# A transformer block on one Trainium2 core: a fifth group of seven-product tiles in the down projection, with its weight sums, sums of products and convolution taps moved to other engines

## The chip, the cores and the metric

The program runs on one core of a Trainium2 chip. The metric is the device time of one execution in microseconds. Time before: 970.25 us, the median of 3 runs (969.86 to 970.68).

In the profile PE is TensorE's matmul, PEld its weight load, DVE is VectorE, ACT is ScalarE, POOL is GpSimd, and SP is the engine that issues most DMAs; a name with q is that engine's queue.

## The reference

One encoder block over x of 256 tokens by 2048 features, in float32: RMSNorm and one input projection, windowed attention of 12 heads beside a Fourier group, an output projection with a residual add, then the feed-forward part, to which the change belongs, and a last RMSNorm:

```python
def _conv_ffn(h, w_up, dw_w, dw_b, w_down):
    up = h @ w_up
    gate, val = up[..., :D_FF], up[..., D_FF:]
    gate = lax.conv_general_dilated(      # centred, width 3, one filter per feature
        gate, dw_w, window_strides=(1,), padding=((CONV_WIDTH // 2, CONV_WIDTH // 2),),
        dimension_numbers=('NWC', 'WIO', 'NWC'), feature_group_count=D_FF) + dw_b
    act = jax.nn.gelu(gate, approximate=False) * val
    return act @ w_down
...
        x = x + _conv_ffn(_rmsnorm(x, norm2_g), w_up, dw_w, dw_b, w_down)
    return _rmsnorm(x, normf_g)
```

D_FF is 5504, which is 43 tiles of 128 features. w_up is 2048 x 11008, w_down 5504 x 2048.

## The kernel before

Every float32 matmul is made of three matmuls on rounded parts. A matrix is split into hi, its value rounded to the matmul type (written by ScalarE), and lo, the rest (raw minus hi, on VectorE); the product sums hi x hi, hi x lo and lo x hi in PSUM. Weights come by DMA in units of 128 x 2048 (1 MB) into three raw buffers, and each unit is split once (`split`, L163 and L164, or `split_product`, L905 and L906 for the groups below). There are three hi and three lo buffers, so unit n+2 is split while unit n is on TensorE.

The feed-forward part is a list of items, made by `ff_items`, that TensorE works off in order. An item of kind gate or val is one up-projection tile (16 k tiles, 32 matmuls, of 512 and 256 columns in turn). A product is 12 matmuls of 512 columns, and a late ("down") item is 24 of them. `ff_step(n)`, called behind the matmuls of item n, issues the work of the other engines in this order: the posts beside item n (those that follow item n-1, and the second step of n-2), then the split of item n+2, then the posts behind item n. All queues run in the order of issue, which is fixed by hand.

The posts of a gate tile: `scaled_sum` (ScalarE copies half of the PSUM result, VectorE adds the other half and multiplies by the token scale r2b), `gate_conv` (ScalarE writes the middle tap and the bias into cv, VectorE adds the two outer taps, L809 and L812), and `gate_gelu` on ScalarE. Of a val tile: `scaled_sum` and `val_mult`, which multiplies by the gate.

The down projection of tiles 0 to 31 is done in 4 groups of 8 tiles by a 2 x 2 block scheme with seven products instead of eight (Strassen's, in the form that needs few sums). The blocks are: two halves of 4 k tiles, two halves of 128 tokens, and output columns c and c+2 of the four column blocks of 512; so each group has two halves c = 0, 1 of 7 products, P1, P2, N3, N4, N5, P6, P7. On the activation side `operand` and `operand_sums` make seven operands per group. On the weight side four blocks a, b, c, d (1 MB each) are loaded into a ring of two buffers (`ring_load`), and sums are made in a buffer x (tag sumw, one buffer): `first_sums` writes x = a+b on VectorE and has a DMA of GpSimd's queue add d onto b in place; after the split of N5 an accumulating DMA adds d onto x, and after P6 another adds c. P1 uses a, P7 b+d, N5 a+b, N3 d, P6 a+b+d, P2 c, N4 a+b+d+c.

The order of products is P1, P7, N5, N3, P6, P2, N4 for c = 0 and P1, N5, P7, N3, P6, P2, N4 for c = 1. PATTERN sets them between the up items of the next 8 tiles: three up items, then product and up item in turn.

`product_out` takes a product out of PSUM on VectorE: it is added onto the output rows xs and onto the shared sums U, N5 and P7 in SBUF, up to two additions for a product. `shared_out`, once per half, folds the shared sums into xs.

Tiles 32 to 39 are done plainly (three matmuls each) by 8 "down" items (LATE), tiles 40 to 42 by the four last items, whose results go through `last_post` (add to xs, square sum). `gain` multiplies by normf_g on GpSimd, `finish` scales by the row norm and stores the output in four pieces for each half of the tokens. PSUM has eight banks: four for up items (mm) and four for products and the rest (dn).

Of the kernel before, what the change touches and what calls it, by code (L numbers as in the profile page):

```python
# [13 lines left out]
P = 128  # L14
# [39 lines left out]
N_GROUPS = 4  # L54
LATE = [list(range(32, 36)), list(range(36, 40))]
# [5 lines left out]
PATTERN = "uuu" + "su" * 13 + "s"  # L61


def ff_items():


    def ups(tiles):
        return [(kind, j) for j in tiles for kind in ("gate", "val")]

    items = ups(range(8))  # L70
    for g in range(N_GROUPS):
        todo = {
            "u": ups(range(8 * g + 8, 8 * g + 16)),
            "s": [("product", g, c, p) for c in range(2) for p in PRODUCTS[c]],
        }
        items += [todo[c].pop(0) for c in PATTERN]
        assert not any(todo.values())
    items += [("down", 0, c) for c in range(4)] + ups(LAST)
    items += [("down", 1, c) for c in range(4)] + [("last", c) for c in range(4)]
    return items  # L80
# [3 lines left out]
def block_kernel(  # L84
# [9 lines left out]
    w_down: bass.AP,  # L94
    w_down_late: bass.AP,
# [25 lines left out]
    for n, it in enumerate(items):  # L121
        if it[0] == "product":
            continue
        up_index[n] = len(units)
        if it[0] in ("gate", "val"):
            units.append((w_up[2 * it[1] + (it[0] == "val")], 2048))
        elif it[0] == "down":
            units.append((w_down_late[4 * it[1] + it[2]], 2048))
        else:
            units.append((w_down_last[it[1]], 512 * len(LAST)))  # L130
# [673 lines left out]
    def gate_conv(j):  # L804
# [4 lines left out]
        nc.vector.scalar_tensor_tensor(  # L809
            cv[:, 1:S], ga[:, 0 : S - 1], w[0], cv[:, 1:S], ALU.mult, ALU.add  # L810
        )
        nc.vector.scalar_tensor_tensor(  # L812
            cv[:, 0 : S - 1], ga[:, 1:S], w[2], cv[:, 0 : S - 1], ALU.mult, ALU.add
        )
# [7 lines left out]
    def val_mult(j):  # L822
        va, ge = sums_of.pop(f"v{j}"), gate_out.pop(j)
        g, q = divmod(j, 8)
        if j >= 8 * N_GROUPS:
            if q % 2 == 0 or j == LAST[0]:
                tag = ("va", "va", "op_P1", "op_N3", "op_P7", "op_N5")[(j - 32) // 2]
                act["pair"] = fp.tile(
                    [P, 2, 512], F32R, tag=tag, name=f"act_{j}", bufs=3 if tag == "va" else 1
                )  # L830
            nc.vector.tensor_tensor(va, va, ge, ALU.mult)
            sums_of[j] = va
            act[j] = act["pair"][:, q % 2, :]
            return
        if q % 4 == 0:
            parts[g, q // 4] = fp.tile(
                [P, 4, S], F32, tag="va", name=f"va{g}k{q // 4}", bufs=3
            )
        nc.vector.tensor_tensor(parts[g, q // 4][:, q % 4, :], va, ge, ALU.mult)
# [18 lines left out]
    def block_of(g, name):  # L858
        k, t = PLACE[name]
        return parts[g, k][:, :, t * P : (t + 1) * P]  # L860

    def operand(g, name):

        o = fp.tile([P, 2, 4, P], F32R, tag=f"op_{name}", name=f"op_{name}", bufs=1)
        a = block_of(g, name)
# [16 lines left out]
    ring, ring_tiles = [(g, c, w) for g in range(N_GROUPS) for c in range(2) for w in "abdc"], {}  # L882
    ring_next = [0]

    def weights_of(g, c, w):
        return w_down[(g * 2 + c) * 4 + "abcd".index(w)]

    def ring_load():
        if ring_next[0] < len(ring):
            key = ring[ring_next[0]]  # L890
            ring_next[0] += 1
            ring_tiles[key] = fp.tile([P, 2048], F32, tag="rawd", name="rawd%d%d%s" % key)
            nc.sync.dma_start(ring_tiles[key], weights_of(*key))

    pending = []

    def split_product(g, c, p):
# [7 lines left out]
        nc.scalar.activation(hi, src, AF.Copy)  # L905
        nc.vector.tensor_tensor(lo, src, f32(hi), ALU.subtract)  # L906
        if p in ("P1", "P7", "N3", "P2"):
            ring_load()
        elif p == "N5":
            nc.gpsimd.dma_start(x, weights_of(g, c, "d"), accum_op=ALU.add)  # L910
        elif p == "P6":
            nc.gpsimd.dma_start(x, weights_of(g, c, "c"), accum_op=ALU.add)
        elif p == "N4" and (g, c) != (N_GROUPS - 1, 1):
            pending.append(lambda: first_sums(g + c, 1 - c))

    def first_sums(g, c):

        a, b = ring_tiles[g, c, "a"], ring_tiles[g, c, "b"]
        x = ring_tiles["x"] = fp.tile([P, 2048], F32, tag="sumw", name=f"sumw{g}{c}", bufs=1)
        nc.vector.tensor_tensor(x, a, b, ALU.add)  # L920
        nc.gpsimd.dma_start(b, weights_of(g, c, "d"), accum_op=ALU.add)

    def split_item(n):
        if n >= len(items):
            return
        it = items[n]
        if n in up_index:
            split(up_index[n])
            if pending:
                pending.pop(0)()  # L930
        else:
            while pending:
                pending.pop(0)()
            split_product(*it[1:])
# [12 lines left out]
    def up_posts(n, kind, j, ps):  # L947
        if kind == "gate":
            at(beside, n + 1, scaled_sum, ps, f"g{j}")
            at(beside, n + 2, gate_conv, j)  # L950
            at(behind, n + 2, gate_gelu, j)
        else:
            at(beside, n + 1, scaled_sum, ps, f"v{j}")
            at(beside, n + 2, val_mult, j)
            if j % 8 == 7 and j < 8 * N_GROUPS:
                g = j // 8
# [9 lines left out]
            if j >= 8 * N_GROUPS:  # L966
# [3 lines left out]
    Z = {}  # L970
    for c in range(2):
        for z in ("U", "N5", "P7"):
            pool, tag = (wp, "junk") if (c, z) == (1, "P7") else (fp, f"z_{z}{c}")
            Z[c, z] = pool.tile([P, 512], F32, tag=tag, name=f"z_{z}{c}", bufs=1)

    def to_out(c, n, t, ps):
        xb = xs[2 * n + c][:, t, :]
        nc.vector.tensor_tensor(xb, ps, xb, ALU.add)

    def to_shared(z, ps, first):  # L980
        if first:
# [298 lines left out]
```

## Time and profile before

| | |
|---|---|
| median of 3 runs | 970.25 us |
| the profiled execution | 969.79 us, of which the span from first to last instruction is 968.0 us |
| mean granted TensorE clock | 0.997 |
| busy in the span | PE 957.5, DVE 757.2, ACT 538.6, POOL 44.5 us |
| moved by DMA | 211.59 MB, mean 219 GB/s |
| feed-forward part | from about 262 us to the end |

Busy time is the time in which an engine had an instruction at work; matmuls overlap, so a busy PE means that one was always under way. A row of a group gives the line, the engine, output and inputs, the count, then busy us and mean ns of one, then the idle time before. A row of the timeline gives start and duration in us.

### The profile page before, as it was taken

Reading aid. Unit: us, or ns where it says so; the run is one execution under the profiler, and the core shown is the slowest. Engines: PE = TensorE matmul, PEld = TensorE weight load, DVE = VectorE, ACT = ScalarE, POOL = GpSimd, SP = SyncE. Lnnn points to the kernel's source line nnn. Section 1 sums busy time; section 2 is a strip of 40 time slices with the busy share of each in tenths; the row PEclk is TensorE's granted clock in tenths of the full one; section 3 lists DMA queues with packets and bytes.
Section 4 is the critical chain, followed back from the end, with each engine's and each line's share of the span. In section 5 each row is a group of like instructions: output and inputs, shape, how many; then the busy total and the mean of one; then the engine's idle time right before and its main releaser. Section 6 shows DMA issues by size and latency. Waiting matters only on the chain.

```text
span 968.0 us, 12817 instructions
## 1 busy us (share of the span) xinstructions
PE 957.5 (99%) x5089; PEld 820.9 (85%) x5089; DVE 757.2 (78%) x942; ACT 538.6 (56%) x656; POOL 44.5 (5%) x59
## 2 busy tenths in 40 slices
PE   9999999999999999999999999999999999999996
PEld 7788888888888888888888888888888888888885
DVE  6668777666666679887898887998889989887765
ACT  6746666555454456656555555565555655554434
POOL 0000000000000000000000000000000000000003
PEclk9999999999999999999999999999999999999998
DMA  8854434455446674977778787777977696766542
GB/s 323 334 184 158 174 131 166 139 174 212 179 174 222 236 238 174 273 248 261 222 256 234 234 288 244 254 223 225 294 244 244 194 295 207 232 238 219 176 131 87
DMA packets 33548, 211.59 MB, mean 219 GB/s; under 512 B 3792, under 2 KB 4304, under 8 KB 9424
## 3 DMA queue, kind: packets, MB, share of 16 engines
q1 hardware_dynamic: 29744, 184.54, 51.5%
q0 software_dynamic: 3600, 26.22, 14.3%
q8 instruction: 40, 0.66, 0.3%
q14 instruction: 20, 0.16, 0.0%
q10 hardware_dynamic: 144, 0.01, 0.0%
HBM read 208.65 MB, written 2.10 MB: 218 GB/s over the span
## 4 chain that ended last, share of the span: by engine, by line
PE 98%; DMA 1%; SPq 0%; ACT 0%; issue 0%; POOL 0%; DVE 0%; ACTq 0%; POOLq 0%
PE ps_gate L313 17%; PE ps_val L313 17%; PE ps_gate L314 8%; PE ps_val L314 8%; PE ps_q L313 5%; PE ps_P L1012 3%; PE ps_P L1014 3%; PE ps_P L1013 3%; PE ps_q L314 2%; PE ps_N L1012 2%; PE ps_N L1014 2%; PE ps_a L304 2%; PE ps_a L302 2%; PE ps_a L303 2%; PE ps_N L1013 2%; PE ps_k L313 2%
## 5 line engine op out<-in xcount | busy, mean ns | idle before, releaser
L164 DVE TENSOR_TENSOR lo<-raw,hi 128x2048 fp32r<-128x2048 f32 (+3 forms) x146 | 314.8, 2156 | 63.0 <-ACT hi L163 63.0
L163 ACT ACTIVATE hi<-raw 128x2048 fp32r<-128x2048 f32 (+3 forms) x145 | 263.1, 1814 | 67.4 <-PE ps_l L303 27.0
L313 PE MATMUL ps_gate<-hU,hi 128*128 128x512 f32 x688 | 242.9, 394 | 0.0
L313 PE MATMUL ps_val<-hU,hi 128*128 128x512 f32 x688 | 242.9, 394 | 0.0
L314 PE MATMUL ps_gate<-hU,lo 128*128 128x256 f32 x688 | 193.1, 281 | 0.0
L314 PE MATMUL ps_val<-hU,lo 128*128 128x256 f32 x688 | 193.1, 281 | 0.0
L313 PEld LDWEIGHTS ps_val<-hU,hi 128*128 128x128 f32 x688 | 129.3, 188 | 30.0
L313 PEld LDWEIGHTS ps_gate<-hU,hi 128*128 128x128 f32 x688 | 129.3, 188 | 30.0
L314 PEld LDWEIGHTS ps_gate<-hU,lo 128*128 128x128 f32 x688 | 129.0, 187 | 1.4 <-DVE lo L164 0.3
L314 PEld LDWEIGHTS ps_val<-hU,lo 128*128 128x128 f32 x688 | 128.9, 187 | 1.3 <-DVE lo L164 0.3
L798 ACT ACTIVATE ft_g<-ps_gate 128x256 f32<-128x256 f32 x43 | 16.5, 383 | 126.3 <-PE ps_gate L314 126.2
L798 ACT ACTIVATE ft_v<-ps_val 128x256 f32<-128x256 f32 x43 | 16.5, 383 | 96.5 <-PE ps_val L314 96.4
L313 PE MATMUL ps_q<-hT,hi 128*128 128x512 f32 x192 | 68.5, 397 | 0.0
L314 PE MATMUL ps_q<-hT,lo 128*128 128x256 f32 x192 | 54.0, 281 | 0.0
L1012 PE MATMUL ps_P<-hi_P,op_P 128*128 128x512 f32 x128 | 50.2, 392 | 0.0
L1014 PE MATMUL ps_P<-lo_P,op_P 128*128 128x512 f32 x128 | 50.1, 391 | 0.0
L1013 PE MATMUL ps_P<-hi_P,op_P 128*128 128x512 f32 x128 | 49.8, 389 | 0.0
L906 DVE TENSOR_TENSOR lo_N<-sumw,hi_N 128x2048 fp32r<-128x2048 f32 x16 | 36.6, 2290 | 10.1 <-ACT hi_N L905 10.1
L313 PEld LDWEIGHTS ps_q<-hT,hi 128*128 128x128 f32 x192 | 36.1, 188 | 8.0
L800 DVE TENSOR_TENSOR fa_g<-ps_gate,ft_g 128x256 f32<-128x256 f32 x43 | 18.1, 422 | 25.8 <-ACT ft_g L798 25.8
L302 PE MATMUL ps_a<-hi,cat 128*128 128x512 f32 x96 | 37.8, 394 | 0.0
L1012 PE MATMUL ps_N<-hi_N,op_N 128*128 128x512 f32 x96 | 37.7, 393 | 0.0
(323 smaller groups left out, 1604.2 us busy)
## 6 DMA issues: line engine op xcount, KB each, us to landing
raw<-in_w_up SPq DMA_DIRECT2D x86, 1024.0 KB, 5.0
raw<-in_w_in SPq DMA_DIRECT2D x21, 1024.0 KB, 4.8
raw<-in_w_out SPq DMA_DIRECT2D x16, 1024.0 KB, 4.8
sumw<-in_w_down POOLq DMA_DIRECT2D x16, 1024.0 KB, 8.5
raw<-in_w_down_late SPq DMA_DIRECT2D x8, 1024.0 KB, 4.8
raw<-in_w_down_last SPq DMA_DIRECT2D x4, 768.0 KB, 4.3
raw<-in_w_in SPq DMA_DIRECT2D x8, 256.0 KB, 6.1
xs<-in_x SPq DMA_DIRECT2D x4, 512.0 KB, 11.1
```

Source lines behind the costliest of these rows:

```text
L163: nc.scalar.activation(hi[:, s], raw[:, s], AF.Copy)
L164: nc.vector.tensor_tensor(lo[:, s], raw[:, s], f32(hi[:, s]), ALU.subtract)
L302: nc.tensor.matmul(ps, ah, wh, start=first and q == q0, stop=False)
L303: nc.tensor.matmul(ps, al, wh, start=False, stop=False)
L304: nc.tensor.matmul(ps, ah, wl, start=False, stop=last and q == q0 + len(kk) - 1)
L313: nc.tensor.matmul(ps, hi[:, s], h, start=k == 0, stop=False)
L314: nc.tensor.matmul(ps[:, 0:S], lo[:, s], h[:, 0:S], start=False, stop=k == NK - 1)
L798: nc.scalar.activation(tmp, ps[:, S : 2 * S], AF.Copy)
L906: nc.vector.tensor_tensor(lo, src, f32(hi), ALU.subtract)
L1012: nc.tensor.matmul(ps, o[:, 0, p, :], hi[:, s], start=p == 0, stop=False)
L1013: nc.tensor.matmul(ps, o[:, 1, p, :], hi[:, s], start=False, stop=False)
L1014: nc.tensor.matmul(ps, o[:, 0, p, :], lo[:, s], start=False, stop=p == 3)
```

## The change

- Groups: GROUPS lists five, the fifth with tiles 32 to 37, that is two halves of 3 tiles. Its weight blocks are 128 x 1536 (`w_down_three`) and its products 9 matmuls. LATE is down to tiles 38 and 39 (four items of 12 matmuls).
- Order: the first three patterns are as before. In the fourth and fifth, some products follow each other directly, and the late items (l) stand between products.
- Weight sums: a+b, and the additions of d after N5 and of c after P6, are tensor_tensor on GpSimd. Only d onto b is still an accumulating DMA. `first_sums` is issued right behind the split of N4, where before it waited for the split of the next up item.
- Products: P1 and N5 of both halves keep a PSUM bank each (`held`) through all groups and are summed there. P6 and P7 go to SBUF sums, P2, N3 and N4 to xs. All other items share the four banks of mm.
- `shared_out` reads the held banks; two of its eight steps are on GpSimd.
- Convolution: `gate_taps` has ScalarE write all three taps; `gate_conv` adds two of them on VectorE as plain tensor_tensor.
- The load of normf_g is issued behind the last P2.
- The end: the first half's output is stored in the order 0, 3, 1, 2, with the last two pieces after the last row norm; the second half's in the order 2, 0, 3, 1.

```diff
-N_GROUPS = 4
-LATE = [list(range(32, 36)), list(range(36, 40))]
+GROUPS = [(0, 4), (8, 4), (16, 4), (24, 4), (32, 3)]
+LATE = [38, 39]
...
-PATTERN = "uuu" + "su" * 13 + "s"
+PATTERNS = ["uuu" + "su" * 13 + "s"] * 3
+PATTERNS += ["uuu" + "sususs" "uss" "us" + "us" "us" "uss" "uss" "us"]
+PATTERNS += ["uuu" + "sususs" "uss" "us" + "us" "us" "llss" "uss" "lls"]
...
-    def gate_conv(j):
+    def gate_taps(j):
         ga = sums_of.pop(f"g{j}")
         w = [vcol(V_DW + 3 * j + i) for i in range(3)]
         cv = fp.tile([P, S], F32, tag="cv", name=f"cv{j}")
         nc.scalar.activation(cv, ga, AF.Identity, bias=vcol(V_DB + j), scale=w[1])
-        nc.vector.scalar_tensor_tensor(
-            cv[:, 1:S], ga[:, 0 : S - 1], w[0], cv[:, 1:S], ALU.mult, ALU.add
-        )
...
+        before = fp.tile([P, S], F32, tag="cv_b", name=f"cv_b{j}", bufs=1)
+        nc.scalar.activation(before, ga, AF.Copy, scale=w[0])
+        behind = fp.tile([P, S], F32, tag="cv_a", name=f"cv_a{j}", bufs=1)
+        nc.scalar.activation(behind, ga, AF.Copy, scale=w[2])
+        gate_out[j] = cv, before, behind
+
+    def gate_conv(j):
+        cv, before, behind = gate_out[j]
+        nc.vector.tensor_tensor(cv[:, 1:S], before[:, 0 : S - 1], cv[:, 1:S], ALU.add)
+        nc.vector.tensor_tensor(cv[:, 0 : S - 1], behind[:, 1:S], cv[:, 0 : S - 1], ALU.add)
         gate_out[j] = cv
...
-        if p in ("P1", "P7", "N3", "P2"):
+        n = 512 * GROUPS[g][1]
+        nc.scalar.activation(hi[:, 0:n], src, AF.Copy)
+        nc.vector.tensor_tensor(lo[:, 0:n], src, f32(hi[:, 0:n]), ALU.subtract)
+        if p == "N5":
+            nc.gpsimd.tensor_tensor(x, x, raw["d"], ALU.add)
+        elif p == "P6":
+            nc.gpsimd.tensor_tensor(x, x, raw["c"], ALU.add)
+        elif p != "N4":
             ring_load()
-        elif p == "N5":
-            nc.gpsimd.dma_start(x, weights_of(g, c, "d"), accum_op=ALU.add)
-        elif p == "P6":
-            nc.gpsimd.dma_start(x, weights_of(g, c, "c"), accum_op=ALU.add)
-        elif p == "N4" and (g, c) != (N_GROUPS - 1, 1):
-            pending.append(lambda: first_sums(g + c, 1 - c))
+        elif (g, c) != (len(GROUPS) - 1, 1):
+            first_sums(g + c, 1 - c)
...
-        nc.vector.tensor_tensor(x, a, b, ALU.add)
+        nc.gpsimd.tensor_tensor(x, a, b, ALU.add)
         nc.gpsimd.dma_start(b, weights_of(g, c, "d"), accum_op=ALU.add)
...
+    held = {(c, p): bank(dn, f"ps_{p}_{c}") for c in range(2) for p in ("P1", "N5")}
...
+    def product_out(g, c, p, ps):
+        tt = nc.vector.tensor_tensor
+        if p in ("P6", "P7"):
+            z = Z[c, p]
+            if g == 0:
+                nc.scalar.activation(z, ps, AF.Copy)
+            else:
+                tt(z, ps, z, ALU.add)
         else:
+            n, t = {"P2": (0, 0), "N3": (1, 0), "N4": (0, 1)}[p]
+            xb = xs[2 * n + c][:, t, :]
+            tt(xb, ps, xb, ALU.add)

     def shared_out(c):
...
+        tt(u, p1, u, ALU.add)
+        tt(x00, p1, x00, ALU.add)
+        tt(w, n5, u, ALU.subtract)
+        gg(u, u, p7, ALU.add)
+        tt(x01, x01, w, ALU.add)
+        tt(w, w, p7, ALU.subtract)
+        gg(x10, x10, u, ALU.add)
+        tt(x11, x11, w, ALU.add)
...
-    outs = finish(0, r3)
+    outs = finish(0, r3, (0, 3, 1, 2))
     next(outs)
     next(outs)
...
-        if p == 0:
-            next(outs)
-    most = most_of(1, 4)
+    r3 = last_scale(1, 4, most_of(1, 4))
     for _ in outs:
         pass
-    for _ in finish(1, last_scale(1, 4, most)):
+    for _ in finish(1, r3, (2, 0, 3, 1)):
         pass
```

More of the change, by code (lines that the diff above doesn't have):

```diff
@@ L954, in up_posts @@
             at(beside, n + 2, val_mult, j)
-            if j % 8 == 7 and j < 8 * N_GROUPS:
-                g = j // 8
+            ends = [first + 2 * half - 1 for first, half in GROUPS]
+            if j in ends:
+                g = ends.index(j)
                 at(behind, n + 1, operand, g, "P1")
@@ L965, in up_posts @@
                 at(behind, n + 7, operand, g, "P6")
-            if j >= 8 * N_GROUPS:
+            if j >= LATE[0]:
                 at(behind, n + 2, act_parts, j)
[L970 to L978, printed above, removed]
@@ L1071, in finish, with load_gain @@
             yield
+    def load_gain():
+        t = fp.tile([P, 2048], F32, tag="sumw", name="gfb", bufs=1)
+        nc.gpsimd.dma_start(t, normf_g.partition_broadcast(P))
+        st["gfb"] = t
     pair = []
```

177 lines of the change are left out of this document (81 added, 96 removed).

## The prediction

> **What bounds the kernel now.** I read the head of the page, its chain, then the kernel by stages, then the order of instructions in the product stages, and last every place where GpSimd computes.
>
> ```profile
> span 968.0 us, 12817 instructions
> PE 957.5 (99%) x5089; PEld 820.9 (85%) x5089; DVE 757.2 (78%) x942; ACT 538.6 (56%) x656; POOL 44.5 (5%) x59
> PE 98%; DMA 1%; SPq 0%; ACT 0%; issue 0%; POOL 0%; DVE 0%; ACTq 0%; POOLq 0%
> ```
>
> The profiled execution took 969.8 us around a span of 968.0, and the median of the runs is 970.25, so a sum against 969.8 stands for either within 0.5 us (a difference under 0.2%, 1.9 us, cannot be told from none). TensorE sets the time: any matmul less is a gain, any gap on it a loss. What could open a gap is VectorE. These are stretches of the four groups of products (start:end, length, then each engine's busy us), as their sum:
>
> ```profile
> sum 495.00, PE 495.00 PEld 424.40 DVE 429.08 ACT 286.93 POOL 20.63; mean PE 123.75 PEld 106.10 DVE 107.27 ACT 71.73 POOL 5.16
> ```
>
> From 371 to 866 us PE is full and DVE has 66 us free, 13%. How near it runs to its deadlines stands in the timeline (start, duration):
>
> ```profile
> 406.46 2.29 DVE L906 TENSOR_TENSOR lo_P<-rawd00c,hi_P 128x2048 fp32r<-128x2048 f32 x1 [0.92 <-ACT hi_P L905]
> 408.67 0.48 DVE L809 SCALAR_TENSOR_TENSOR cv<-fa_g,vec,cv 128x255 f32<-128x255 f32 x1
> ...
> 409.58 0.69 DVE L984 TENSOR_TENSOR z_U<-ps_P,z_U 128x512 f32<-128x512 f32 x1
> 410.18 2.28 DVE L164 TENSOR_TENSOR lo<-raw,hi 128x2048 fp32r<-128x2048 f32 x1
> ...
> 414.79 2.29 DVE L906 TENSOR_TENSOR lo_N<-sumw,hi_N 128x2048 fp32r<-128x2048 f32 x1 [0.92 <-ACT hi_N L905]
> 417.00 0.42 DVE L839 TENSOR_TENSOR va1k<-fa_v,cv 128x256 f32<-128x256 f32 x1
> 417.34 0.69 DVE L978 TENSOR_TENSOR xs<-ps_P,xs 128x512 f32<-128x512 f32 x1
> 417.94 2.28 DVE L164 TENSOR_TENSOR lo<-raw,hi 128x2048 fp32r<-128x2048 f32 x1
> ```
>
> and the first matmul of each item in the same stretch:
>
> ```profile
> 406.79 0.40 PE L313 MATMUL ps_val<-hU,hi 128*128 128x512 f32 x1
> ...
> 412.37 0.39 PE L1012 MATMUL ps_P<-hi_P,op_P 128*128 128x512 f32 x1
> ...
> 415.12 0.40 PE L313 MATMUL ps_gate<-hU,hi 128*128 128x512 f32 x1
> ...
> 423.45 0.40 PE L313 MATMUL ps_val<-hU,hi 128*128 128x512 f32 x1
> ```
>
> An up item (gate or val) lasts 412.37 - 406.79 = 5.58 us on PE, a product 415.12 - 412.37 = 2.75 us, 0.229 a matmul. The lo made at 410.18 ends at 412.46 and is wanted at 415.12, the one at 417.94 ends at 420.22 and is wanted at 423.45: margins of 2.66 and 3.23 us. An item's lo is made two items ahead and no earlier (three hi/lo buffers), so a delay of DVE beyond some 3 us stops PE.
>
> **The change part by part.** *Fewer matmuls.* Tiles 32 to 37 cost 6 x 24 = 144 matmuls as plain k tiles and 14 products x 9 = 126 as a group: 18 x 0.229 = 4.1 us off PE, all on the path. The weights of a product of this group are 1536 wide.
>
> *Work taken from DVE.*
>
> ```profile
> L920 DVE TENSOR_TENSOR sumw<-rawd11a,rawd11b 128x2048 f32<-128x2048 f32 x1 | 2.3, 2284 | 0.0
> L812 DVE SCALAR_TENSOR_TENSOR cv<-fa_g,vec,cv 128x255 f32<-128x255 f32 x43 | 20.8, 484 | 1.5
> L164 DVE TENSOR_TENSOR lo<-raw,hi 128x1536 fp32r<-128x1536 f32 x4 | 7.0, 1758 | 4.1 <-ACT hi L163 4.1
> L255 ACT ACTIVATE qT<-add_q 128x256 fp32r<-128x256 f32 x12 | 5.0, 416 | 4.8 <-DVE add_q L569 4.8
> ```
>
> Eight first sums go (8 x 2.28 = 18.3). Eight tensor_tensor of 0.69 (409.58) per group and half (six in group 0, where ScalarE copies) become five: in the first four groups 58 become 36, 15 us. The two taps become plain adds, as the val product at 417.00 (0.42 for 0.48), twice for 43 gates: 5 us. All this is off the path as long as PE is fed. ScalarE takes two taps per gate at about 0.42 (the nearest row, a scaled copy of this size): 0.84 in 16.7 us, with ACT busy 287 of 495, hidden. P1 and N5 keep four PSUM banks for good, so everything else turns through the other four; an item's bank is read one item later and wanted four later, hidden while DVE is not over one item late. If it were, that delay itself would be the price, and it is in the stalls below.
>
> *The sums on GpSimd.* Each group and half has three: a+b after the split of N4, +d after N5, +c after P6. The accumulating DMAs of +d and +c go; that of b stays, issued behind a+b on GpSimd's queue.
>
> ```profile
> sumw<-in_w_down POOLq DMA_DIRECT2D x16, 1024.0 KB, 8.5
> L432 POOL TENSOR_TENSOR sq_a<-sq_a,sq 128x256 f32<-128x256 f32 x11 | 8.1, 738 | 87.3 <-ACT sq L431 87.3
> L1032 POOL TENSOR_TENSOR xs<-xs,gfb 128x512 f32<-128x512 f32 x6 | 7.6, 1293 | 91.6 <-ACT junkc L1025 91.6
> ```
>
> From 738 ns at 256 columns and 1293 at 512, a column costs 2.17 ns, so 2048 take 4.62 us and 1536 take 3.51. As a wait it fits: the next use of the sum is two items or more away, and b, with 8.5 us more, is wanted by P7, which stands third in the second half and behind three extra up items in a new group. SP's queue sees a ring load wait for a sum at N3 and P2, a few us, with three raw buffers ahead of it. But the same rows show what a GpSimd add does to DVE:
>
> ```profile
> 104.70 0.74 POOL L432 TENSOR_TENSOR sq_a<-sq_a,sq 128x256 f32<-128x256 f32 x1 [4.14 <-ACT sq L431]
> 105.14 0.69 DVE L653 TENSOR_TENSOR pt<-ps_t,pt 128x512 fp32r<-128x512 f32 x1 [1.00 <-ACT pt L652]
> 105.75 0.41 DVE L256 SCALAR_TENSOR_TENSOR qT<-add_q,qT 128x256 fp32r<-128x256 f32 x1
> ...
> 112.20 0.74 POOL L432 TENSOR_TENSOR sq_a<-sq_a,sq 128x256 f32<-128x256 f32 x1 [6.76 <-ACT sq L431]
> 112.46 0.76 DVE L256 SCALAR_TENSOR_TENSOR qT<-add_q,qT 128x256 fp32r<-128x256 f32 x1 [0.81 <-ACT qT L255]
> ...
> 958.58 1.27 POOL L1032 TENSOR_TENSOR xs<-xs,gfb 128x512 f32<-128x512 f32 x1 [1.14 <-ACT junkc L1025]
> 958.60 1.54 DVE L1065 TENSOR_SCALAR y<-xs,rstd 128x512 f32<-128x512 f32 x1
> 962.60 0.48 DVE L1065 TENSOR_SCALAR y<-xs,rstd 128x512 f32<-128x512 f32 x1
> ```
>
> qT from two SBUF tensors takes 0.41 us alone and 0.76 under a GpSimd add, ending 0.28 after it; the tensor_scalar takes 0.48 alone and 1.54, ending 0.29 after the add. DVE made no headway under them. The one with an operand in PSUM (105.14) kept its 0.69. All lo splits, taps, val products, operands and the r2b scaling have two SBUF operands; only outputs from PSUM and the first half of scaled_sum do not. So each sum, once it runs, holds DVE's main work for 4.62 us; and what lets it start is the end of a lo split, when DVE has a full queue behind that split.
>
> Price by deadline. Behind a split before which a gate ran (N5 and P6 and N4 of the first half, N5 of the second): it ends at 417.08, DVE runs the val product to 417.42, GpSimd takes the port to 422.0, PSUM work goes on, the next lo ends 2.15 later (0.13 of its start-up passes in waiting, as above) at 424.2, wanted at 423.45: about 0.7 late, 0.55 with GpSimd's own start-up overlapped. [...] Behind a split before which a val ran (P6 and N4 of the second half): 408.75, one tap to 409.1, port until 413.7, the other tap, the PSUM output and the lo: 416.8, wanted at 415.12: 1.7, taken as 1.5. The first N5 of a group meets the operands:
>
> ```profile
> 513.00 0.69 DVE L867 TENSOR_TENSOR op_P<-va1k,op_P 128x512 fp32r<-128x512 f32 x1
> ```
>
> It stands right behind the split of N5 and has two SBUF operands, so 0.69 comes on top, and DVE is later there by the operands before it (a few more rows of this kind), taken as the same again: 2.0. A group then costs 3 x 0.55 + 2.0 + 2 x 1.5 = 6.65, three groups 20. The bounds are 4 and 9 a group: without the start-ups and with a split held twice.
>
> Group 3 has pairs of products in a row. P6's lo ends 2.3 before P6 starts, and P2's is wanted 2.75 after that, 5.0 in all, against 4.62 + 2.2: 1.8 late. So is the up item behind N4 (1.8), 1.3 at the last N4 (a 1536 sum), and five smaller ones of 0.1 to 0.6: 7.5 (4 to 11).
>
> Group 4 on PE: 10 ups, 14 products of 9 matmuls and 4 late items of 12, 55.8 + 28.8 + 11.0 = 95.6 us. On DVE: 10 x 2.29 + 14 x 1.76 + 4 halves of 2.29 for splits (52), ups 15, outputs 18 at 0.69 (12), the first shared_out (six, 4), operands and act parts 8, first of the last splits 3: 94. It has no room, and six sums hold it 6 x 3.51 = 21, of which some 6 pass under PSUM work and 5 in waits: 10 (5 to 16).
>
> *The end.* The second shared_out, six tensor_tensor of 0.69 on DVE, now falls beside the last products. It stands ahead of last_post(0, 0), 4.1 us; the third last product wants a bank that it frees, and the last split stands behind it: 1.5 on PE (0, if all of it lies under idle time, to 4).
>
> ```profile
> 947.21 2.55 POOL L1032 TENSOR_TENSOR xs<-xs,gfb 128x512 f32<-128x512 f32 x2 [87.21 <-ACT junkc L1025]
> ...
> 958.83 0.28 PE L1168 MATMUL ps_e<-lo,act 128*128 128x256 f32 x1
> ...
> 960.06 0.41 DVE L1037 TENSOR_TENSOR xs<-ps_e,xs 128x256 f32<-128x256 f32 x1
> ```
>
> The new output order takes the 1.54 tensor_scalar from before the last sum, which waited 0.95 behind the last matmul (959.11 to 960.06); two outputs are now behind it, so 0.7 of it is gained (0 to 0.95). The load of normf_g, 1 MB, now waits for the buffer x until the split of the last N4, some 2 us ahead of the last products; at the 8.5 us of a load on this queue it lands about 7 us into them. The first gain ran 11.6 us before the last matmul (947.21), so its successors have room to move up behind it; were they late, the pieces that they scale would be, by at most 2 us.
>
> Sum: -4.1 - 0.7 + 20 + 7.5 + 10 + 1.5 = +34.2, so 969.8 becomes 1004. With all bounds 12 + 4 + 5 + 0 to 27 + 11 + 16 + 4, and the tail's 0 to 0.95, that is 986 to 1024.
>
> As a check: DVE in the first four groups does 429 - 18 - 15 - 4 = 392 us, and 24 holds of 4.62 are 111, of which about 17 pass under PSUM work: 486 of 495, and the waits for ACT hi (0.92 at each product) no longer fit.
>
> **Rivals.** *Faster: GpSimd comes second.* In no row did a GpSimd add arrive while DVE was at work on two SBUF operands. If DVE, whose instructions start 0.08 us before the one ahead has ended, keeps the port until its queue runs dry, the add begins behind the next up lo (420.22) and falls on the scaling and a product's lo, which has 3.62 of margin (408.75 to 412.37) besides the waits. It decides where the add starts later than 2.5 us behind the split, or lasts under 2.9 us (4.62 less the 1.7 above). Then no stall but a few in group 4: 969.8 - 4.8 + 0 to 3 = 965 to 968. Against it: a PSUM output follows within 0.4 to 0.9 us of most splits, and in that time GpSimd can begin. [...] *Half held.* The add lets DVE in between pieces of it: stalls remain only in pairs and in group 4, a third to a half of 39: 978 to 985. The 1.27 us hold without headway speaks against it. *DVE becomes the bound.* Then late work adds up instead of being made good in the next item: 486 and the 56 waits of 0.92 are 537 us, 42 over the stage, and with group 4 and the end 969.8 - 4.8 + 42 + 10 + 1.5 = 1019. For it speaks the check above, against it that a wait for ACT shrinks as DVE runs late.
>
> **How the numbers follow.** Holds as worked out 0.60, DVE as the bound 0.10, half held 0.09, faster 0.18, holds and gains that cancel 0.03. The likeliest case's own range is 986 to 1024. The range goes from 965, the lower edge of the faster case, to 1020, above which lies half of the case with DVE as the bound and a little of the likeliest: with what may fall under 965, some 0.15 to 0.2 are left out. Faster 0.18, same 0.03, slower 0.79.
>
> **What would show it.** Right: POOL rows of 128x2048 at about 4.6 us, DVE lo rows of up to 7 us where they meet one (2.29 now), PE gaps of 0.5 to 2 us named for DVE lo, and 174 matmuls where 192 were. Wrong: lo rows all at 2.29 and POOL rows stretched or late; then the port goes to DVE and the time is near 965. A shorter tail shows as the last sum starting at the end of the last matmul.

## The result, and the profile after

The changed kernel takes 1011.12 us (median of 6 runs, 1010.21 to 1012.41) against 970.08 for the kernel before on the same chip: a ratio of 1.0422, 95% interval 1.0409 to 1.0436, or 41 us slower. The profiled execution took 1010.5 us around a span of 1008.7.

The head of its page and the first line of its chain:

```profile
span 1008.7 us, 12909 instructions
...
PE 965.3 (96%) x5071; PEld 816.1 (81%) x5071; DVE 845.0 (84%) x929; ACT 580.0 (58%) x751; POOL 177.2 (18%) x79
...
PE 60%; DVE 25%; issue 7%; ACT 5%; DMA 1%; POOL 1%; POOLq 0%; ACTq 0%; SPq 0%; DVEq 0%
```

Before, the chain was 98% PE. Now a quarter of it is DVE, although 18 matmuls went (5089 to 5071) and DVE has 13 instructions fewer. It was busy for 757.2 us and is for 845.0; POOL went from 44.5 to 177.2. The windows of the stages (start:end, length, then the busy us of PE, PEld, DVE, ACT, POOL) are groups 0 to 2, group 3, group 4, and the last products:

```profile
371.00:773.00 402.00, 388.07 (x2044) 328.75 (x2043) 370.52 (x321) 237.13 (x261) 93.31 (x24) 1.00 0.59 204
773.00:869.00 96.00, 90.79 (x459) 75.16 (x457) 90.95 (x70) 56.58 (x58) 28.97 (x8) 1.00 0.52 181
869.00:976.00 107.00, 99.35 (x495) 82.12 (x494) 103.07 (x106) 57.92 (x69) 22.99 (x10) 0.98 0.53 174
976.00:998.70 22.70, 17.81 (x83) 13.66 (x81) 18.24 (x23) 8.29 (x17) 10.66 (x9) 1.00 0.15 61
```

PE, which in the kernel before was busy for all of 371 to 866, has lost 14 us in the first, 5 in the second, 8 in the third and 5 in the last. This is where, on POOL and then on DVE (start, duration), in group 0:

```profile
385.49 5.00 POOL L916 TENSOR_TENSOR sumw<-sumw,rawd00d 128x2048 f32<-128x2048 f32 x1 [57.94 <-DVE lo_N L914]
403.28 4.74 POOL L918 TENSOR_TENSOR sumw<-sumw,rawd00c 128x2048 f32<-128x2048 f32 x1 [12.79 <-DVE lo_P L914]
...
438.93 5.73 POOL L916 TENSOR_TENSOR sumw<-sumw,rawd01d 128x2048 f32<-128x2048 f32 x1 [12.47 <-DMA rawd01d<-in_w_down]
```

```profile
385.31 0.68 DVE L873 TENSOR_TENSOR op_N<-va0k,op_N 128x512 fp32r<-128x512 f32 x1
385.91 4.86 DVE L844 TENSOR_TENSOR va1k<-fa_v,cv 128x256 f32<-128x256 f32 x1
390.69 2.28 DVE L168 TENSOR_TENSOR lo<-raw,hi 128x2048 fp32r<-128x2048 f32 x1
...
403.45 0.68 DVE L993 TENSOR_TENSOR xs<-ps_N,xs 128x512 f32<-128x512 f32 x1
404.06 6.12 DVE L168 TENSOR_TENSOR lo<-raw,hi 128x2048 fp32r<-128x2048 f32 x1
...
435.35 2.29 DVE L914 TENSOR_TENSOR lo_N<-sumw,hi_N 128x2048 fp32r<-128x2048 f32 x1 [0.48 <-ACT hi_N L913]
...
437.89 2.28 DVE L168 TENSOR_TENSOR lo<-raw,hi 128x2048 fp32r<-128x2048 f32 x1
441.88 0.42 DVE L804 TENSOR_TENSOR fa_g<-ps_gate,ft_g 128x256 f32<-128x256 f32 x1 [1.70 <-ACT ft_g L802]
442.33 2.62 DVE L805 TENSOR_TENSOR fa_g<-fa_g,r2b 128x256 f32<-128x256 f32 x1
```

A val product of 0.42 us takes 4.86 and ends 0.28 behind the GpSimd add; a lo of 2.29 takes 6.12 and ends 2.16 behind it, which is its own work. So in these rows a DVE instruction with two SBUF operands that starts under a GpSimd add gets nowhere until the add ends: I call this a hold. The output from PSUM at 403.45 keeps its 0.68. What that does to PE is in the waits of the matmuls (idle time and its releaser in brackets):

```profile
393.03 0.39 PE L318 MATMUL ps_val<-hU,lo 128*128 128x256 f32 x1 [1.75 <-DVE lo L168]
...
410.23 0.39 PE L318 MATMUL ps_val<-hU,lo 128*128 128x256 f32 x1 [0.26 <-DVE lo L168]
```

I measure a gap as what an item takes beyond its undisturbed length (5.585 us for an up item, 2.745 and 2.06 for products of 12 and 9 matmuls): 7.61 and 6.16 us for these two. From the first group to the last matmul the gaps add up to 42.9 us: 18.1 in groups 0 to 2, 8.2 in group 3, 10.5 in group 4, 6.0 in the last products. A gap holds the wait and what PE loses behind it: here 1.6 us of the 10.5 are matmuls that ran at a lower clock (0.50 for 3.41 us) behind the longest wait (2.38 us; more of this below, with the sums alone). The tail is the time from the end of the last matmul to the end of the span: 10.0 us, for 8.9 before.

### The profile page after: what moved, and what is told of

It is laid out like the page before. It is cut to its first block, busy times and chain, and to the rows that moved or that the text cites. A ratio compares the mean times of both kernels' runs of the same rounds, so it can differ in the third digit from the quotient of the medians.

```text
span 1008.7 us, 12909 instructions
## 1 busy us (share of the span) xinstructions
PE 965.3 (96%) x5071; PEld 816.1 (81%) x5071; DVE 845.0 (84%) x929; ACT 580.0 (58%) x751; POOL 177.2 (18%) x79
## 4 chain that ended last, share of the span: by engine, by line
PE 60%; DVE 25%; issue 7%; ACT 5%; DMA 1%; POOL 1%; POOLq 0%; ACTq 0%; SPq 0%; DVEq 0%
DVE lo L168 10%; PE ps_gate L317 10%; PE ps_val L317 10%; PE ps_val L318 6%; PE ps_gate L318 5%; PE ps_q L317 4%; DVE lo_P L914 4%; PE ps_q L318 2%; ACT hi_P L913 2%; PE ps_a L308 2%; PE ps_a L306 2%; PE ps_a L307 2%; DVE lo_N L914 2%; PE ps_k L317 1%; ACT hi_N L913 1%
## 5 line engine op out<-in xcount | busy, mean ns | idle before, releaser
L168 DVE TENSOR_TENSOR lo<-raw,hi 128x2048 fp32r<-128x2048 f32 (+3 forms) x142 | 337.7, 2378 | 53.9 <-ACT hi L167 53.7
L167 ACT ACTIVATE hi<-raw 128x2048 fp32r<-128x2048 f32 (+3 forms) x141 | 251.8, 1786 | 44.2 <-PE ps_a L307 13.4
L318 PEld LDWEIGHTS ps_val<-hU,lo 128*128 128x128 f32 x688 | 129.0, 187 | 18.1 <-DVE lo L168 17.6
L1015 PE MATMUL ps_P<-lo_P,op_P 128*128 128x512 f32 x152 | 59.7, 393 | 1.7 <-DVE lo_P L914 1.7
L1013 PE MATMUL ps_P<-hi_P,op_P 128*128 128x512 f32 x152 | 59.6, 392 | 0.0
L1014 PE MATMUL ps_P<-hi_P,op_P 128*128 128x512 f32 x152 | 59.2, 390 | 0.0
L812 ACT ACTIVATE cv<-fa_g,vec 128x256 f32<-128x256 f32 x43 | 25.6, 596 | 45.2 <-DVE fa_g L805 45.2
L914 DVE TENSOR_TENSOR lo_N<-sumw,hi_N 128x2048 fp32r<-128x2048 f32 (+1 forms) x20 | 43.6, 2181 | 5.7 <-ACT hi_N L913 5.5
L822 DVE TENSOR_TENSOR cv<-cv_a,cv 128x255 f32<-128x255 f32 x43 | 43.7, 1016 | 4.8 <-DVE cv L821 0.5
L1015 PE MATMUL ps_N<-lo_N,op_N 128*128 128x512 f32 x114 | 45.0, 395 | 2.6 <-DVE lo_N L914 2.5
L1013 PE MATMUL ps_N<-hi_N,op_N 128*128 128x512 f32 x114 | 44.7, 392 | 0.0
```

Source lines behind the costliest of these rows:

```text
L167: nc.scalar.activation(hi[:, s], raw[:, s], AF.Copy)
L168: nc.vector.tensor_tensor(lo[:, s], raw[:, s], f32(hi[:, s]), ALU.subtract)
L318: nc.tensor.matmul(ps[:, 0:S], lo[:, s], h[:, 0:S], start=False, stop=k == NK - 1)
L812: nc.scalar.activation(cv, ga, AF.Identity, bias=vcol(V_DB + j), scale=w[1])
L822: nc.vector.tensor_tensor(cv[:, 0 : S - 1], behind[:, 1:S], cv[:, 0 : S - 1], ALU.add)
L914: nc.vector.tensor_tensor(lo[:, 0:n], src, f32(hi[:, 0:n]), ALU.subtract)
```

## The experiments

Theory 1 is the prediction's: a GpSimd add holds VectorE's work on two SBUF operands, started by the end of a split, and the lo behind it comes too late. The rivals to it are named in each expectation: that the denser order, or the load on VectorE as such, leaves no room whoever makes the sums, and that four PSUM banks are too few for all that turns through them.

**The sums as before.** In the changed kernel the three sums go back to a+b on VectorE and accumulating DMAs.

```diff
-            nc.gpsimd.tensor_tensor(x, x, raw["d"], ALU.add)
+            nc.gpsimd.dma_start(x, weights_of(g, c, "d"), accum_op=ALU.add)
...
-        nc.gpsimd.tensor_tensor(x, a, b, ALU.add)
+        nc.vector.tensor_tensor(x, a, b, ALU.add)
```

> The changed kernel, with the weight sums done as before the change: a+b on VectorE behind the next up split, +d and +c by accumulating DMAs. All else of the change stays. Theory 1 (each GpSimd sum holds VectorE for its 4.6 us, just when VectorE has a full queue): the stalls of the three even groups go (2.0 + 0.6 + 0.5 + 1.5 + 1.5 in each, 18 in all), as do most in groups 3 and 4; what is left is the end (6.0 on TensorE beside the last products) and DMA sums that are late between close products (2 to 5 us): about 976 us (971 to 982). Theory 2 (the denser order of items, with the taps on ScalarE, leaves no room on VectorE whoever makes the sums) or theory 3 (four PSUM banks for all the rest are too few): it stays above 995.

Measured 979.86 us, ratio 1.0103 (1.0086 to 1.0120). Its window of groups 0 to 2:

```profile
371.00:770.00 399.00, 399.00 (x2124) 342.60 (x2123) 332.37 (x344) 248.91 (x274) 16.61 (x19) 1.00 0.78 245
```

PE is full again, with the same order, taps and banks. 11.9 us of gaps are left, all in group 3 (1.9), group 4 (4.9) and the end (5.0): 31 of the 41 us were the sums. It also says how much of the gaps of the later groups the sums made: some 6 of 8.2 us in group 3, and 5.5 of 10.5 in group 4.

**All three sums on VectorE.** The same edit with `nc.vector.tensor_tensor` in all three places, so VectorE does more and GpSimd makes none of the sums.

> The changed kernel, with all three sums as tensor_tensor on VectorE at the same places (30 more instructions there, 24 of 2.29 us and 6 of 1.76, none on GpSimd). Theory 1: a sum now costs VectorE 2.2 us in place of a hold of 4.6, which the margins of the even groups take (2.2 + 0.34 + 0.6 + 2.2 = 5.4 of the 6.4 us to the next deadline, 5.9 where the taps come first), so only group 4 (10 us over) and the end (6) remain: 988 us (980 to 995). Theory 2: VectorE has 63 us more of its own work, so it is slower than the changed kernel or no faster: 1005 or more.

Measured 979.16 us, ratio 1.0088 (1.0073 to 1.0103), below the range that I gave. The same window:

```profile
371.00:770.00 399.00, 399.00 (x2123) 342.53 (x2122) 358.34 (x353) 249.09 (x274) 5.22 (x6) 1.00 0.62 214
```

DVE does 26 us more than with the DMAs and PE loses nothing. So in these groups neither this load on VectorE nor the accumulating DMAs matter; a GpSimd add costs more than the same add on VectorE itself, 4.62 us of hold against 2.28 of work.

**The sums later.** The GpSimd sums stay, but each starts behind the split of the next up item, through a two-column GpSimd add that reads that lo.

```diff
+            if pending:
+                lo = f32(halves[up_index[n]][1])
+                nc.gpsimd.tensor_tensor(after_lo, lo[:, 0:2], lo[:, 0:2], ALU.add)
+                pending.pop(0)()
```

> The changed kernel, with the same sums on GpSimd, but in the even order each starts only behind the next up split (a small GpSimd add reads that split's lo first); between products that follow each other directly nothing is delayed. The amount of work and of hold is the same; only the moment moves. Theory 1, with the price set by the deadline of the next lo: the 18 us of the even groups go, and a few in groups 3 and 4: 989 us (983 to 997). The rival that VectorE is bound by the sum of its work and the holds: no change, 1005 to 1013.

Measured 993.20 us, ratio 1.0235 (1.0220 to 1.0250). The sums last as long, and what they hold now is the scaling ahead of a product's lo (rows of POOL and DVE):

```profile
402.16 4.62 POOL L923 TENSOR_TENSOR sumw<-sumw,rawd00c 128x2048 f32<-128x2048 f32 x1
```

```profile
402.29 4.76 DVE L805 TENSOR_TENSOR fa_g<-fa_g,r2b 128x256 f32<-128x256 f32 x1
406.98 2.28 DVE L917 TENSOR_TENSOR lo_P<-rawd00c,hi_P 128x2048 fp32r<-128x2048 f32 x1
```

Gaps in groups 0 to 2 fall from 18.1 to 5.9 us, in the other stages they stay (7.7, 10.5, 6.1). DVE is busy, its held time included, for 384.00 of the 399.00 us from 371 to 770. So what a hold costs depends on where it starts; its length was the same. Of the 18 us gained, 12.6 are gaps; most of the rest, 3.9 us, stands ahead of the groups (this kernel's up items there last 5.55 us, those of the others 5.65, and the feed-forward part starts 2 us earlier), and its cause is open. The start of that part lies between 260.9 and 263.7 us in all profiles of the case.

**The sums alone.** The kernel before with the three sums on GpSimd and nothing else.

> The kernel before, with one part of the change alone: its three sums per group and half as GpSimd tensor_tensor right behind the splits of N4, N5 and P6. Theory 1: four even groups at 6.1 to 7.5 us each, 24 to 30: 994 to 1000 us. Theories 2 and 3 (order of items, banks, taps): no more than 2 us from 970.

Measured 1012.44 us, ratio 1.0429 (1.0413 to 1.0445): as slow as the whole change, and 12 to 18 us above what I expected. Its gaps add up to 40.7 us. The places where it loses more than the changed kernel are the first N5 of each group (2.7, 4.6, 6.0 and 5.0 us, for 2.0) and the N5 of the last half (6.7). DVE at the second of them:

```profile
514.44 0.69 DVE L984 TENSOR_TENSOR z_U<-ps_P,z_U 128x512 f32<-128x512 f32 x1
515.04 0.68 DVE L978 TENSOR_TENSOR xs<-ps_P,xs 128x512 f32<-128x512 f32 x1
...
522.04 4.84 DVE L839 TENSOR_TENSOR va2k<-fa_v,cv 128x256 f32<-128x256 f32 x1
526.80 0.68 DVE L984 TENSOR_TENSOR z_P<-ps_P,z_P 128x512 f32<-128x512 f32 x1
```

Ahead of the hold stand the two outputs of P1, 1.4 us; where P1 and N5 stay in PSUM they are not there. The matmul that needs the lo waits 2.98 us, for 1.74 in the changed kernel. The rest is clock. These are PE behind that wait, and the window of these 3.3 us (its third number from the end is the granted clock):

```profile
529.73 0.58 PE L314 MATMUL ps_val<-hU,lo 128*128 128x256 f32 x1 [2.98 <-DVE lo L164]
530.11 0.63 PE L313 MATMUL ps_val<-hU,hi 128*128 128x512 f32 x1
530.54 0.41 PE L314 MATMUL ps_val<-hU,lo 128*128 128x256 f32 x1
530.76 0.63 PE L313 MATMUL ps_val<-hU,hi 128*128 128x512 f32 x1
```

```profile
529.70:533.00 3.30, 3.27 (x11) 2.83 (x12) 3.27 (x4) 2.40 (x2) 0.00 (x0) 0.55 0.69 218
```

A pair of matmuls takes 0.65 us (530.11 to 530.76) and not the 0.35 of 32 matmuls in 5.58; the wider one lasts 0.63 for 0.40. Behind the four longest waits of this kernel (2.96 to 4.10 us) matmuls run at the low clock for 2.9 to 6.1 us, which costs about 8 us in all. So two things were missing in my expectation: work that is free while VectorE has time counts in full once a hold has made it late (read from this trace; no run takes the two outputs away alone), and a long wait can cost clock as well, as each of these four did.

**The relief alone.** The kernel before with held banks, the new shared_out and the taps on ScalarE, sums and order untouched.

> The kernel before with two parts of the change alone: P1 and N5 summed in held PSUM banks, with all other items in the banks of mm and the new shared_out, and the taps on ScalarE with plain additions on VectorE. Sums, groups, order and outputs as before. Some 20 us of work leave VectorE in the four groups. Theory 1 (all of it was hidden, and four banks for the rest are enough): 970.4 us (969.5 to 971.5), the same. Rival (the shared banks or the second shared_out with its two GpSimd steps stop TensorE): 972 us or more.

Measured 972.58 us, ratio 1.0023 (1.0014 to 1.0031): 2.2 us more, as the rival had it. The 12 us less of DVE in groups 0 to 2 (344.33 to 332.33) win nothing, and four banks are enough there (PE is busy for all of it). Two gaps, of 0.7 and 1.3 us, stand behind the GpSimd steps of the two shared_out. At the second (0.69 alone):

```profile
874.71 1.66 DVE L1005 TENSOR_TENSOR sum<-sum,z_P 128x512 f32<-128x512 f32 x1
876.40 1.67 DVE L1007 TENSOR_TENSOR xs<-xs,sum 128x512 f32<-128x512 f32 x1
```

**The end.** The end of the changed kernel, first the matmuls of the last products that waited, then DVE:

```profile
982.32 0.47 PE L306 MATMUL ps_e<-hi,act 128*128 128x512 f32 x1 [2.00 <-DVE xs L1001]
987.64 0.47 PE L306 MATMUL ps_e<-hi,act 128*128 128x512 f32 x1 [1.00 <-DVE xs L1040]
990.43 0.50 PE L306 MATMUL ps_e<-hi,act 128*128 128x512 f32 x1 [0.47 <-ACT hi L167]
992.53 0.51 PE L308 MATMUL ps_e<-lo,act 128*128 128x512 f32 x1 [1.36 <-DVE lo L168]
```

```profile
980.88 0.69 DVE L1000 TENSOR_TENSOR z_P<-ps_P,z_P 128x512 f32<-128x512 f32 x1
...
983.53 1.67 DVE L1005 TENSOR_TENSOR sum<-sum,z_P 128x512 f32<-128x512 f32 x1
985.23 1.66 DVE L1007 TENSOR_TENSOR xs<-xs,sum 128x512 f32<-128x512 f32 x1
986.82 1.27 DVE L1040 TENSOR_TENSOR xs<-ps_e,xs 128x512 f32<-128x512 f32 x2
990.41 2.06 DVE L168 TENSOR_TENSOR lo<-raw,hi 128x1536 fp32r<-128x1536 f32 x1 [2.32 <-ACT hi L167]
...
998.34 1.75 DVE L1064 SCALAR_TENSOR_TENSOR y<-xs,rstd,gfb 128x512 f32<-128x512 f32 x1 [1.12 <-POOL rstd L1057]
1000.01 0.74 DVE L1040 TENSOR_TENSOR xs<-ps_e,xs 128x256 f32<-128x256 f32 x2
```

Shared_out begins at 980.88, and the last lo comes 9.5 us later: it waits for its hi, which ScalarE writes at 988.91, behind the square sums of the two sums of 986.82. First, four last products take free PSUM banks of mm:

```diff
-        ps = bank(dn, f"ps_e{c}{b}")
+        free = (c, b) in ((1, 0), (1, 1), (2, 0), (3, 0))
+        ps = bank(mm if free else dn, f"ps_e{c}{b}")
```

> The changed kernel with one line more: four of the last products take their PSUM bank from the four of mm, which are free, and not from those that hold P1 and N5 of the second half until the second shared_out has read them. In the changed kernel the third last product waits from 979.93 to 982.32 us for such a bank, the fifth from 986.25 to 987.64. Theory 1 (the end is late because of VectorE's queue: the split of the last weights at 990.41 waits for a hi that ScalarE writes behind two square sums, which wait for two sums on VectorE at 986.8, behind eight steps of shared_out): the products move up but then wait for that lo at the same time as before, so 1010.5 to 1011.5 us, no gain beyond 0.5. Rival (the held banks cost the time): the two waits of 2.4 and 1.4 us go, 1007 to 1008 us.

Measured 1011.41 us, ratio 1.0419 (1.0405 to 1.0433), no gain. The products run ahead and stop at the hi and lo of the last weights, for longer, and come out of it at a lower clock (0.80 for the 0.47 above); the tail is 2 us shorter, so the sum is the same:

```profile
990.88 0.80 PE L306 MATMUL ps_e<-hi,act 128*128 128x512 f32 x1 [4.07 <-ACT hi L167]
992.95 0.79 PE L308 MATMUL ps_e<-lo,act 128*128 128x512 f32 x1 [0.84 <-DVE lo L168]
```

The bank was the first wait, the late split the one that counts. Next, with these banks, the eight steps of the second shared_out (now all on VectorE) are spread over four items from behind the last P2, the split of the last weights stands ahead of last_post, and VectorE, not GpSimd, scales the last piece but one:

```diff
+            if end and (c, p) == (1, "P6"):
+                for k, f in enumerate(shared_steps(c)):
+                    at(behind, n + 2 + k // 2, f)
...
     ff_step(n)
+    split(i + 3)
     last_post(0, 0, held_ps)
...
-    gain(2, 1)
```

> The changed kernel, weight sums on GpSimd as they are, with its end rearranged: four last products in banks of mm; the eight steps of the second shared_out, all on VectorE, issued two at a time from behind the last P2 on, where P6 is out, and not all at once behind the last N4; the split of the last weight unit issued ahead of the first two last_post; and no gain on GpSimd for the last piece but one, whose output is scaled by both factors on VectorE. Theory 1 (the end cost 6.0 us of gaps and 1.1 of tail, because shared_out and the late split stand in VectorE's queue at one place and a GpSimd gain holds an output): gaps of the last products 6.0 to 0 to 1.5 us, tail from 10.05 to about 8.3, that is 1011.1 - 5 - 1.7 = 1004.5 us (1003 to 1007). Rival (VectorE has no room ahead of the last products either, so the eight steps cost the same wherever they stand): the gaps move to the items before, and only the tail is won, 1009 to 1010 us.

Measured 1008.28 us, ratio 1.0384 (1.0369 to 1.0400): less than half of the gain that theory 1 said. The gaps of the last products fall from 6.0 to 0.4 us, as it had it. The other stages keep theirs or grow a little (group 4 has 11.4 for 10.5, and in this profile one wait of group 0 cost 1.6 of clock). But the tail, from the end of the last matmul to the end of the span, grows from 10.0 to 11.5: the sums of the last products are now done in a row, so five gains run in a row on GpSimd ahead of the row norm.

**All of it together.** Sums as before the change, the end as above, and the first shared_out spread as well.

> The version whose sums are made as before the change (a+b on VectorE, the rest by accumulating DMA), which took 979.9 us, with the rearranged end and with the first shared_out also issued two steps at a time, on VectorE alone. Theory 1: of its 11.9 us of gaps 4.9 stand in the last products and some 3 at the first shared_out, and 1.9 in the tail: 979.9 - 4.4 - 1.5 - 1.8 = 972 us (970 to 975), even with the kernel before within a few us and not clearly better, as group 3 and the dense order of group 4 keep some 4. Rival (VectorE has no room in group 4): 976 to 979 us.

Measured 973.97 us, ratio 1.0040 (1.0027 to 1.0053). Of 11.9 us of gaps 4.7 are left. Its gains on GpSimd, and the two DVE instructions behind them:

```profile
955.86 6.27 POOL L1042 TENSOR_TENSOR xs<-xs,gfb 128x512 f32<-128x512 f32 x5 [15.49 <-ACT junkc L1035]
```

```profile
962.71 0.75 DVE L1072 SCALAR_TENSOR_TENSOR y<-xs,rstd,gfb 128x512 f32<-128x512 f32 x1 [2.36 <-POOL rstd L1064]
963.38 0.75 DVE L1047 TENSOR_TENSOR xs<-ps_e,xs 128x256 f32<-128x256 f32 x2
```

The last matmul ended at 960.54; its sum starts 2.8 us later behind an output that waits for the norm. The next kernel scales one more piece on VectorE (four gains are left on GpSimd), puts the first outputs behind the last sums, and issues the outputs of groups 3 and 4 and of the late items behind the next split:

```diff
-                at(beside, n + 1, product_out, g, c, p, ps)
+                at(behind if g >= 3 else beside, n + 1, product_out, g, c, p, ps)
...
-            at(beside, n + 1, down_out, c, ps)
+            at(behind, n + 1, down_out, c, ps)
```

> The version with sums by DMA and rearranged end, which took 974.0 us, with three more steps. Outputs of products of groups 3 and 4 and of the late items are issued behind the next split, not ahead of it (4.1 of its 4.7 us of gaps stand where two splits follow with such an output between them). The third column block of both halves is scaled by normf_g on VectorE, so GpSimd has four gains, not six, ahead of the row norm (its tail went from 10.1 to 11.4 us, as five gains in a row, 6.27 us, stood ahead of the norm). The first two outputs stand behind the last sums. Theory 1: gaps 4.7 to 1.5, tail 11.4 to 8.5, so 974.0 - 3.2 - 2.9 = 968 us (966.5 to 970), 2 below the kernel before: the 4.1 us of the 18 matmuls, less what is left of gaps. Rival (the outputs issued later hold up PSUM banks, and the gaps stay): 971 us, even with before.

Measured 980.03 us, ratio 1.0108 (1.0090 to 1.0126): the rival's wait, and more of it than it said. The tail falls from 11.5 to 9.6 us, but the gaps grow from 4.7 to 12.5, as products and late items now wait for banks whose output comes late:

```profile
924.95 0.77 PE L1020 MATMUL ps_P<-hi_P,op_P 128*128 128x512 f32 x1 [3.83 <-DVE xs L1029]
945.48 0.50 PE L306 MATMUL ps_l<-hi,act 128*128 128x512 f32 x1 [1.04 <-DVE xs L999]
```

**The order of the last outputs alone,** on the kernel before.

> The kernel before with the new order of the last outputs alone. In its trace a tensor_scalar of 1.54 us (0.48 alone), held by a gain on GpSimd, stood ahead of the last sum, which started 0.95 us behind the last matmul. Theory 1: that is gained, 0.7 of the 8.9 us from the end of the last matmul to the end of the span, 969.6 us (969.2 to 970.2), within what can be told from no change. Rival (in the new order the gain holds the output that now stands there, y of c=3, as in the changed kernel, where it took 1.75 us for 0.74): no gain or 0.4 us more, 970.3 to 970.9 us.

Measured 969.81 us, ratio 0.9997 (0.9988 to 1.0006), which cannot be told from no change. In its trace the term can be seen, though:

```profile
957.45 0.74 DVE L1061 SCALAR_TENSOR_TENSOR y<-xs,rstd,gfb 128x512 f32<-128x512 f32 x1
958.11 0.42 DVE L1037 TENSOR_TENSOR xs<-ps_e,xs 128x256 f32<-128x256 f32 x1
958.99 0.42 DVE L1037 TENSOR_TENSOR xs<-ps_e,xs 128x256 f32<-128x256 f32 x1 [0.46 <-PE ps_e L1168]
```

The last sum starts with the end of the last matmul (958.96), and the tail is 8.4 us for 8.9.

No version here beats the kernel before. In the best one the 4.1 us of the 18 matmuls are given back by gaps, most of them in groups 3 and 4 with their pairs of products and few up items between them (4.7 us with the end), and a longer tail (11.5 us for 8.9) comes on top.

## Why the prediction was right, and where its terms were off

The forecast was 1004 us and the measurement 1011.1, inside the range and inside that of the likeliest case. The mechanism, holds priced by the deadline of the next lo, is what the runs show, and it makes 31 of the 41 us. Term by term, from the two profiles (their spans differ by 40.7 us):

| term | predicted | measured |
|---|---|---|
| 18 matmuls | -4.1 | -4.1 |
| groups 0 to 2 | 20 (12 to 27) | 18.1 |
| group 3 | 7.5 (4 to 11) | 8.2 |
| group 4 | 10 (5 to 16) | 10.5 |
| last products | 1.5 (0 to 4) | 6.0 |
| tail | -0.7 (-0.95 to 0) | +1.15 |
| start of the feed-forward part | 0 | +0.8, scatter |

*Where luck helped.* In groups 3 and 4 the totals agree better than the working. I put all of 7.5 and 10 down to the sums, but with the sums as before 1.9 and 4.9 us are left there, and with the sums on VectorE 0.9 and 6.0, so the holds made some 6 to 7 and 4.5 to 5.5. In group 4 I had weighed work against time; the trace has a few waits, and 4.3 us of it is one of them with its clock.

*The holds.* The first N5 costs 2.0 in each group as worked out; P6 and the first N4 0.53 to 0.57 for 0.55; P6 and N4 of the second half 1.44 to 1.52 for 1.5. The second half's N5 was wrong: 0.55 predicted, nothing measured. I let the split of N5 start that sum, but the trace names the DMA of raw d as what it waited for (438.93). It comes 1.3 us later than the end of the split (the lo of 435.35), while DVE is in the next lo, and GpSimd waits for the end of that lo (5.73 us for 4.62) and then works mostly in DVE's idle time; the 2.62 us scaling has its slack.

*The length of the sums.* 4.62 us predicted and 4.61 to 4.62 measured where nothing held them up (402.16, in the kernel with later sums).

*Who comes second.* The rival "GpSimd comes second" needed an add that arrives during DVE work; 438.93 is one, and it lasted 5.73 with the lo at its 2.28. (I wrote that no row of the kernel before had this; one add there, at 72.10, starts in the last 0.13 us of such an instruction, too short an overlap to decide anything.) So that order exists and here cost PE nothing, as the rival said, but it took an add that was late, and the splits that start the others are followed by an output from PSUM or by another short instruction, behind which GpSimd gets in (the adds of 385.49 and 403.28 took 5.00 and 4.74 us). So the trace has both orders: under these two adds the DVE instruction that came later was held (4.86 us for 0.42, 6.12 for 2.29), and during the lo of 437.89 the add that came later (5.73 for 4.62). What the prediction calls the port stands for this hold; what causes it, no trace shows.

*Half held* falls with the 4.86 us val product: no headway under the add. *DVE as the bound* (1019) falls with the kernel whose sums start later: the same holds fill 384 of 399 us of DVE there, and PE loses a third of what it did. The check of 486 of 495 us was a little high (461 busy in 498; the waits for ACT's hi_P and hi_N fell from 34.8 to 16.0 us), and the load it gives is not what set the time.

*A slip.* Group 0 has five outputs on VectorE per half in the kernel before, not six; the 58 was worked out with five.

*The end* is the term that failed. I priced shared_out as its six steps on VectorE, 4.1 us, less what lies under idle time, and named both the bank and the split behind it, but took 1.5 and a bound of 4; it measured 6.0. What I left out: the last split stands behind two last_post and, on ScalarE, behind their square sums, so a late shared_out delays hi and lo of the last weights in full, and its two GpSimd steps hold DVE for another 2 us (1.67 and 1.66 for 0.69 each, at 983.53 and 985.23). The kernel with free banks shows that the split decides; with spread steps and an earlier split together the gaps go (6.0 to 0.4), and no run has one of these two alone.

*The tail.* The gain from the order is there in other kernels (8.4 us of tail with the order alone, 8.1 in the kernel with free banks). In the changed kernel GpSimd's gain of the last piece but one met the output of c=3 (1.75 for 0.74 at 998.34), and the last sum started 1.4 us behind the last matmul: the same hold as in the kernel before, on another instruction.

*Hidden work.* The taps took 0.50 us each on ScalarE for an assumed 0.42, and were hidden. The relief of DVE was rightly costed at nothing by itself (972.6, and that with 2 us of gaps behind GpSimd steps), but beside the sums it was not nothing: in groups 0 to 2, where the order of items is the same, the gaps are 26.2 us without it and 18.1 with it; some 4 us of the difference are clock.

*The clock.* My sum had one speed for PE. That was nearly right for the change itself, whose waits are mostly under 2 us (1.6 us lost to the lower clock in group 4), and about 8 us wrong for the sums alone.

## What to carry to other kernels

Before moving an elementwise step from VectorE to GpSimd, ask not how long it takes there but what VectorE has in its queue when it starts: here an add of 2.28 us became 4.62 us in which VectorE got only its work on PSUM done (0.68 us an output), and the same add left on VectorE cost nothing in groups 0 to 2 (PE busy for 399.00 of 399 us). If it has to be GpSimd, start it where VectorE's next work with two SBUF operands has slack; the same sums one split later cost a third in groups 0 to 2. And an engine with 13% to spare is no cover for a hold that is longer than its margin to the next deadline.

## What the runs showed of the hardware

- Behind each of the longest waits PE came back at half speed. In the changed kernel the granted clock was 0.50 for 3.41 us behind the wait of 2.38 us that ended at 946.96, and 1.00 behind the one of 2.00 us at 982.32; in the sums alone a pair of matmuls took 0.65 us for 0.35 behind the wait of 2.98. Between the first group and the last matmul the granted clock of all profiles is low in thirteen stretches, at 0.50 for 3.41 us in ten and for 6.83 us in three. They followed each of the seven waits of 2.64 to 4.10 us, four of eight between 2.00 and 2.41, and two shorter ones (1.36 and 1.76). Why waits of one length fall on both sides was not shown.
- An add that reached GpSimd 1.04 us into a DVE lo took 1.11 us longer (5.73 us for 4.62), and the lo kept its 2.28.
- A GpSimd add of 512 columns between two SBUF tensors cost the DVE instruction beside it 0.97 us (1.66 for 0.69), one of 2048 columns 3.8 to 4.4 us (6.12 for 2.29, 4.86 for 0.42), and an output from PSUM nothing (0.68 beside the add at 403.28).
- Accumulating DMAs for the same sums (216.3 MB in all against 196.4, 245 GB/s in groups 0 to 2) cost PE nothing in those groups (busy for 399.00 of 399 us).
